# When the taps of the long convolutions enter VectorE's queue: a count of its work in place of a fixed rate

## The chip, the cores and the metric

The kernel runs on one core of a Trainium2 chip. The metric is device time in microseconds (us), the time of one execution; the kernel before was timed three times. A profile of one more execution shows what each engine did.

## What is computed

A decoder trunk of two layers over 1024 positions of 1024 channels, all in float32. Each layer is, cut to what matters here:

```python
h = rmsnorm(x, norm_g)
a_val, a_glu, a_z, qkv, b_z, b_beta, b_alpha, c_u, c_v, c_z, gates = split(h @ w_in)
a   = causal_dwconv(a_val * sigmoid(a_glu), a_dw) + a_dw_b     # 31 taps, 512 channels
y_a = silu(layernorm(a)) * silu(a_z)
q, k, v = split(silu(causal_dwconv(qkv, b_conv)))              # 4 taps, 3072 channels
y_b = rmsnorm(gated_delta_rule(l2norm(q), l2norm(k), v, b_beta, b_alpha)) * silu(b_z)
y_c = gelu(c_u) * spatial_mix(layernorm(gelu(c_v))) * silu(c_z)
merged = sum(sigmoid(gate_i) * (y_i @ proj_i) for i in (a, b, c))
x = x + merged @ w_out
```

## The kernel before

Channels lie on the 128 partitions, positions along the free dimension. A layer has two large parts. The first, which the change touches, makes most of the projection h @ w_in and, beside it, the convolutions and norms. The second runs the delta rule, the remaining gate tiles and the output projections; its code is not touched.

**Pairs, groups, steps.** The first part is the generator `pairs` (L326). A pair is two tiles of 128 projected columns by all 1024 positions, made with Winograd's form of Strassen's method: seven products of half size instead of eight. There are 31 pairs a layer, counted from 0 here. One product is a group: twelve matmuls of 128x512 (four slices of the inner dimension, each in three passes of high and low parts), written to one PSUM tile `ps` of a pool of four (`pg`). Three matmuls with one slice are a step, so a pair has 28 steps; the generator yields after each. After a group, VectorE adds `ps` to the pair's output tiles `o1`, `o2` (L364, one or two adds of 128x512), or ScalarE copies it (L360), and so frees the buffer. After the last group of a pair its `use` function works on the outputs: Tanh and a 1024-wide product for the A branch's GLU (`use_glu`, L1322 and L1323), Silu and two 1024-wide products for the `z` gates (`both` L717, `mul_free` L1137), or the start of a convolution.

**Weights.** Each product needs a weight tile in high and low parts: ScalarE copies the high part (L173), GpSimd subtracts to get the low part (L174) and forms the sums of weights (L287, L298). A buffer for them comes free when TensorE has done the group that used it.

**Convolutions.** The class `Convs` (L652 on) keeps a list of convolutions. A job is one half (512 positions) of one tile: ScalarE begins the running sum in PSUM (L1057 or L706), VectorE adds one tap at a time (L686, the operation called a tap here), ScalarE ends it (L1059 or L708). A tile of the A branch has 60 taps, one of q, k or v 6; 384 a layer. The call `todo.tap()` puts one tap into VectorE's queue.

**What sets the order.** In this part VectorE's and TensorE's instructions stand in the order in which the program writes them (L1414). ScalarE, GpSimd and SyncE are ordered by the scheduler, which estimates when an instruction's inputs are ready. The function `interleave` advances `pairs` by a step and, at steps written down by hand, side generators: the C norm (`c_norm`, `to_norm` L1100 on) and C mix, the gate scalars (`gate_scalars`, L590 on), the A norm (`a_norm`, L1078 on). One norm tile is: TensorE transposes (L1106), VectorE takes statistics (L1067 to L1071), GpSimd an inverse root (L1073), VectorE a small product (L1075), ScalarE the normalising itself (L1109); the transposes back (L1088) or the mix (L1124) follow.

**When a tap is written.** After each step `pairs` adds a credit and writes a tap for each whole credit: 0.65 a step, or 0.5 in the four pairs named as slow (pairs 2, 3, 22 and 23, where the norms run). If there is no convolution at hand, the credit is spent for nothing. So with work at hand the rate is 18.2 taps a pair, whatever else VectorE has to do.

Of the kernel before, what the change touches and what calls it, by code (L numbers as in the profile page):

```python
# [45 lines left out]
S_A_NORM = 8, 5  # L46
S_HEAD = -4, 1
S_NEXT = 50, 61, 77, 76, 74
TAPS_FAST, TAPS_SLOW = 0.65, 0.5
EXTRA = 2  # L50
AT_YC = -20
LAG_DMA, LAG_POOL = 4, 5
# [18 lines left out]
def hybrid_trunk_kernel(ctx: ExitStack, tc: tile.TileContext, x, norm_g, w_in, a_dw, a_dw_b,  # L71
                        a_ln_g, a_ln_b, a_proj, b_conv, b_a_log, b_dt_bias, b_onorm_g, b_proj,
                        c_ln_g, c_ln_b, c_ws, c_bs, c_proj, w_out, final_g, out):
    nc = tc.nc
    PSUM = bass.MemoryType.PSUM
    pe, act, dve, pool, sp = nc.tensor, nc.scalar, nc.vector, nc.gpsimd, nc.sync

    const = ctx.enter_context(tc.tile_pool(name="const", bufs=1))
    prm = ctx.enter_context(tc.tile_pool(name="prm", bufs=1))
# [20 lines left out]
    def F(*ts):  # L100
        for t in ts:
            free.append(held.pop(id(t))[0])
# [220 lines left out]
        made("S4", s2)  # L323
        yield

    def pairs(specs, blk, todo, slow):  # L326

        ws = [{} for _ in specs]
        made = chain(*(blocks(srcs, w, w is ws[-1]) for (srcs, _), w in zip(specs, ws)))
# [3 lines left out]
        with tc.issue_after(last_pow[0].ins), tc.issue_after(last_x[0].ins):  # L333
            for _ in range(len(wfree)):
                make()
        step, credit = 0, 0.0
        for (_, use), w in zip(specs, ws):
            o1, o2 = U("o1"), U("o2")
            c11, c12, c21, c22 = (o[:, h * HALF:(h + 1) * HALF] for o in (o1, o2) for h in range(2))
            last = w is ws[-1]  # L340
            for nm, nb in LAST_STEPS if last else STEPS:
                ps = pg.tile([P, HALF], F32, name="ps")
                wt = w.pop(nm)
                for k in range(4):
                    for i, (wi, ri) in enumerate(PASSES):
                        pe.matmul(ps, lhsT=wt[:, wi, k, :], rhs=blk(nb, ri, k),  # L346
                                  start=(k == 0 and i == 0), stop=(k == 3 and i == 2))
                    step += 1
                    credit += TAPS_SLOW if step // 28 in slow else TAPS_FAST
                    while credit >= 1:  # L350
                        todo.tap()
                        credit -= 1
                    yield
                FW(wt)
                if last:
                    drop_sum(nb)
                with tc.high_priority():
                    alone = dict(A11=c11, S2=c21, A22=c22) if last else dict(A11=c11)
                    if nm in alone:
                        act.activation(out=alone[nm], in_=ps, func=AF.Copy)  # L360
                    else:
                        for out, other in SUMS[nm]:
                            out, other = (dict(C11=c11, C12=c12, C21=c21, C22=c22)[c] for c in (out, other))
                            dve.tensor_tensor(out=out, in0=other, in1=ps, op=ALU.add)  # L364
                    early = {"A11": c11, "S1": c22}.get(nm)
                    if last and early is not None:
                        dve.tensor_tensor(out=c21, in0=c21, in1=early, op=ALU.add)
                    if nm == "S4":
                        use(o1, o2)
                make()  # L370
# [764 lines left out]

    def mul_free(y, u):
        dve.tensor_tensor(out=y, in0=y, in1=u, op=ALU.mult)  # L1137
        F(u)

    def y_rhs(ys):  # L1140
# [140 lines left out]
    def layer(l, before, ws=None, parts=1):  # L1281
# [38 lines left out]
        def use_glu(c):  # L1320
            def use(o1, o2):
                act.activation(out=o1, in_=o1, func=AF.Tanh, scale=0.5)  # L1322
                dve.scalar_tensor_tensor(out=o1, in0=o1, scalar=1.0, in1=o2, op0=ALU.add, op1=ALU.mult)  # L1323
                F(o2)
                a_conv(todo, l, c, o1)
            return use
# [35 lines left out]
        at = {}  # L1362
# [49 lines left out]
        def at_step(nm, d, gap):  # L1412
            return at[nm] * 28 + d, gap
        tc_dve = tc.manual_schedule(engines={mybir.EngineType.DVE})  # L1414
        tc_dve.__enter__()
        slow = (at["c_mix"], at["c_mix"] + 1, at["a_norm"], at["a_norm"] + 1)
        interleave(pairs(specs, block_rhs, todo, slow),
                   [(late(lambda: c_norm(gvs)), *at_step("c_norm", *S_C_NORM)),
                    (late(lambda: c_mix(l, gvs, ys, gus)), *at_step("c_mix", *S_C_MIX)),
                    (late(lambda: gate_scalars(l, r)), *at_step("scalars", *S_SCALARS)),  # L1420
# [177 lines left out]
```

## Time and profile before

| what | value |
|---|---|
| time, median of 3 runs | 2700.17 us (2697.55 to 2701.52) |
| the profiled execution, time | 2699.63 us |
| the profiled execution, span of the core | 2697.9 us |
| mean granted TensorE clock | 0.988 of full speed |
| TensorE matmuls busy | 2576.4 us (95%) |
| VectorE busy | 1653.7 us (61%) |
| ScalarE busy | 1256.4 us (47%) |
| GpSimd busy | 1423.2 us (53%) |

The span runs from the first to the last instruction; the execution's own time is 1.7 us longer. Busy shares are means over parts of the program that differ: the first part of the first layer lies at about 64 to 729 us, that of the second layer at about 1402 to 2060 us. Matmuls follow each other before the one ahead has ended, so their busy times overlap, and the ends are modelled. In a row, PE is TensorE, PEld its weight load, DVE VectorE, ACT ScalarE, POOL GpSimd; "[2.74 <-ACT o L717]" means that the engine was idle for 2.74 us before, and what ended that.

### The profile page before, as it was taken

The page shows a single profiled execution, that of the slowest core. Times are in us where ns is not written, and L with a number is a line of the kernel's source. Part 1 is how long each engine was busy: PE and PEld are TensorE (multiplying, and loading weights), DVE is VectorE, ACT ScalarE, POOL GpSimd, SP SyncE. Part 2 cuts the span into 40 slices and gives each one's busy share as a digit, 9 for nine tenths or more (in the row PEclk, how much of TensorE's full clock was granted, in tenths as well). Part 3 has the DMA queues.
Part 4 walks back from the last instruction along what each step waited for, and adds up shares of the span by engine and source line. Part 5 has one row for each costly group of instructions (what it writes and reads, how often), then busy time and mean ns, then how long its engine had stood idle before and what let it go on. Part 6 is the DMA issues. An engine that isn't in the chain of part 4 may idle for free.

```text
span 2697.9 us, 42676 instructions
## 1 busy us (share of the span) xinstructions
PE 2576.4 (95%) x15963; PEld 2120.3 (79%) x15963; DVE 1653.7 (61%) x2934; ACT 1256.4 (47%) x2996; POOL 1423.2 (53%) x1144
## 2 busy tenths in 40 slices
PE   7899999999899999999999989999998999999998
PEld 6687778878778888788867877888786888877887
DVE  6688998666545453445276888986564545444442
ACT  4433435565556666322134333365654666652221
POOL 7767667767533332363167767676674334224520
PEclk9999999999999999999999999999999999999999
DMA  4122233434544535554312223343446344445432
GB/s 156 47 63 86 87 94 119 139 102 121 178 113 116 146 103 157 184 168 134 117 65 55 71 72 93 94 157 102 125 123 178 104 132 122 123 150 183 156 125 78
DMA packets 361635, 319.65 MB, mean 118 GB/s; under 512 B 98930, under 2 KB 313556, under 8 KB 360404
## 3 DMA queue, kind: packets, MB, share of 16 engines
q1 hardware_dynamic: 361428, 316.92, 38.8%
q8 instruction: 126, 2.06, 0.3%
q14 instruction: 81, 0.66, 0.1%
HBM read 221.12 MB, written 95.75 MB: 117 GB/s over the span
## 4 chain that ended last, share of the span: by engine, by line
PE 79%; DVE 9%; ACT 4%; POOL 3%; DMA 3%; issue 2%; SPq 0%; DVEq 0%; POOLq 0%; ACTq 0%
PE ps L346 35%; PE ps L246 24%; PE ps L1261 6%; PE pa L753 1%; DVE pr L686 1%; PE ps L270 1%; DMA wr<-in_w_in_dram 1%; PE pr L986 1%; PE pr L1003 1%; PE pr L995 1%; POOL S L174 1%; PE pr L1012 1%; DVE nm L1075 1%; DMA gam<-gc_d 1%; PE pa L802 1%
## 5 line engine op out<-in xcount | busy, mean ns | idle before, releaser
L174 POOL TENSOR_TENSOR S<-st,S 128x512 fp32r<-128x512 f32 x248 | 330.6, 1333 | 192.7 <-ACT S L173 192.4
L346 PE MATMUL ps<-hT,A 128*128 128x512 f32 x1488 | 366.0, 394 | 0.0
L686 DVE SCALAR_TENSOR_TENSOR pr<-o,dwT,pr 128x512 f32<-128x512 f32 (+7 forms) x480 | 356.9, 745 | 13.6 <-ACT pr L1057 3.4
L364 DVE TENSOR_TENSOR o<-o,ps 128x512 f32<-128x512 f32 x430 | 287.1, 681 | 116.2 <-PE ps L346 105.9
L174 POOL TENSOR_TENSOR wl<-wr,wh 128x512 fp32r<-128x512 f32 (+2 forms) x164 | 198.5, 1224 | 293.6 <-PE ps L246 138.7
L246 PE MATMUL ps<-hT,wh 128*128 128x512 f32 x960 | 334.4, 429 | 0.0
L346 PEld LDWEIGHTS ps<-hT,A 128*128 128x128 f32 x1488 | 280.9, 190 | 59.0 <-issue 0.8
L173 ACT ACTIVATE S<-st 128x512 fp32r<-128x512 f32 x248 | 156.6, 631 | 359.0 <-PE ps L346 205.0
L174 POOL TENSOR_TENSOR A<-wr,A 128x512 fp32r<-128x512 f32 x186 | 248.8, 1338 | 23.6 <-ACT A L173 23.1
L686 DVE SCALAR_TENSOR_TENSOR pr<-o,cvT,pr 128x512 f32<-128x512 f32 (+3 forms) x288 | 211.7, 751 | 43.3 <-ACT pr L706 39.0
L346 PE MATMUL ps<-T,A 128*128 128x512 f32 x744 | 187.6, 400 | 17.3 <-DVE o L364 17.2
L246 PE MATMUL ps<-hT,wl 128*128 128x512 f32 x480 | 189.5, 395 | 0.0
L346 PE MATMUL ps<-hT,S 128*128 128x512 f32 x744 | 183.8, 392 | 0.0
L346 PEld LDWEIGHTS ps<-T,A 128*128 128x128 f32 x744 | 142.0, 193 | 49.7 <-issue 20.3
L173 ACT ACTIVATE A<-wr 128x512 fp32r<-128x512 f32 x186 | 116.9, 629 | 119.9 <-PE ps L346 109.0
L346 PE MATMUL ps<-T2h,S 128*128 128x512 f32 x496 | 168.4, 397 | 3.0 <-ACT T2h L173 3.0
L346 PE MATMUL ps<-T3h,S 128*128 128x512 f32 x496 | 166.3, 393 | 4.2 <-ACT o L360 4.2
L346 PE MATMUL ps<-T1h,S 128*128 128x512 f32 x496 | 165.2, 392 | 0.0
L173 ACT ACTIVATE wh<-wr 128x512 fp32r<-128x512 f32 (+2 forms) x164 | 85.6, 549 | 165.3 <-issue 123.4
L246 PEld LDWEIGHTS ps<-hT,wh 128*128 128x128 f32 x960 | 151.1, 190 | 11.6
L346 PEld LDWEIGHTS ps<-hT,S 128*128 128x128 f32 x744 | 137.8, 188 | 28.5 <-issue 0.8
L1261 PE MATMUL ps<-woh,mg 128*128 128x512 f32 x512 | 140.7, 391 | 0.0
(298 smaller groups left out, 5732.4 us busy)
## 6 DMA issues: line engine op xcount, KB each, us to landing
wr<-in_w_in_dram SPq DMA_DIRECT2D x160, 512.0 KB
g_d<-gth SPq DMA_DIRECT2D x32, 512.0 KB
g_d<-o SPq DMA_DIRECT2D x16, 512.0 KB
z_d<-o SPq DMA_DIRECT2D x16, 512.0 KB
v_d<-o SPq DMA_DIRECT2D x16, 512.0 KB
k_d<-o SPq DMA_DIRECT2D x16, 512.0 KB
q_d<-o SPq DMA_DIRECT2D x16, 512.0 KB
gam<-gc_d SPq DMA_DIRECT2D x16, 512.0 KB
```

The lines of the kernel that those rows point to most:

```text
L173: act.activation(out=hi, in_=src, func=AF.Copy)
L174: lo_eng.tensor_tensor(out=lo, in0=src, in1=hi.bitcast(F32), op=ALU.subtract)
L246: pe.matmul(ps[h], lhsT=w[wi][:, k, :], rhs=rhs(h, ri, k), start=(k == 0 and i == 0), stop=(k == kt - 1 and i == 2))
L270: pe.matmul(ps[h][:, sl], lhsT=w[wi][:, k, :], rhs=rhs(h, ri, k)[:, sl], start=(k == 0 and i == 0), stop=(k == kt - 1 and i == 2))
L346: pe.matmul(ps, lhsT=wt[:, wi, k, :], rhs=blk(nb, ri, k), start=(k == 0 and i == 0), stop=(k == 3 and i == 2))
L364: dve.tensor_tensor(out=out, in0=other, in1=ps, op=ALU.add)
L686: dve.scalar_tensor_tensor(out=acc[:, lo:], in0=x[:, h * HALF + lo - s:(h + 1) * HALF - s], scalar=taps[s - 1], in1=acc[:, lo:], op0=ALU.m ...
L753: pe.transpose(tp[:, j * P:(j + 1) * P], src[:, half * 4 + j, :], ident)
L802: pe.matmul(tp[:, j], lhsT=kT[:, n], rhs=qT[:, n], start=True, stop=True)
L986: pe.matmul(ks, lhsT=kT[:, n], rhs=st, start=True, stop=True)
L995: pe.matmul(pz, lhsT=zt[:, n, :], rhs=rt, start=True, stop=True)
L1261: pe.matmul(ps[h], lhsT=mg[hh, ri, k // 4][:, k % 4, off:off + P], rhs=wo[k][wi][:, h * HALF:(h + 1) * HALF], start=(k == 0 and i == 0), s ...
```

## The change

The credit goes. In its place the program keeps a count, `queued`, of how much work in us stands in VectorE's queue, by its own reckoning. Every VectorE instruction that is written adds a cost by its kind: 0.68 for a tensor_tensor, 0.75 for a scalar_tensor_tensor (a tap is one), 0.7 for statistics, 0.3 for a reduction, 0.2 for others. The two kinds of 1024-wide products add 1.4 more. Each step of TensorE takes 0.7 off, down to no less than -1.5. Taps are written as long as the count is at or below zero, so at most three at once, and none while other work is counted. The distinction of slow pairs goes too. The count works while the program is built; no instruction is added or removed.

```diff
--- before.py
+++ after.py
@@ -46,7 +46,7 @@
 S_A_NORM = 8, 5
 S_HEAD = -4, 1
 S_NEXT = 50, 61, 77, 76, 74
-TAPS_FAST, TAPS_SLOW = 0.65, 0.5
+STEP_US, IDLE_US, WIDE_US = 0.7, 1.5, 1.4
 EXTRA = 2
 AT_YC = -20
 LAG_DMA, LAG_POOL = 4, 5
@@ -73,7 +73,18 @@
                         c_ln_g, c_ln_b, c_ws, c_bs, c_proj, w_out, final_g, out):
     nc = tc.nc
     PSUM = bass.MemoryType.PSUM
-    pe, act, dve, pool, sp = nc.tensor, nc.scalar, nc.vector, nc.gpsimd, nc.sync
+    pe, act, pool, sp = nc.tensor, nc.scalar, nc.gpsimd, nc.sync
+
+
+    queued = [0.0]
+    COST = dict(tensor_tensor=0.68, scalar_tensor_tensor=0.75, tensor_reduce=0.3, bn_stats=0.7)
+
+    class Counted:
+        def __getattr__(self, name):
+            queued[0] += COST.get(name, 0.2)
+            return getattr(nc.vector, name)
+
+    dve = Counted()
 
     const = ctx.enter_context(tc.tile_pool(name="const", bufs=1))
     prm = ctx.enter_context(tc.tile_pool(name="prm", bufs=1))
@@ -323,7 +334,7 @@
         made("S4", s2)
         yield
 
-    def pairs(specs, blk, todo, slow):
+    def pairs(specs, blk, todo):
 
         ws = [{} for _ in specs]
         made = chain(*(blocks(srcs, w, w is ws[-1]) for (srcs, _), w in zip(specs, ws)))
@@ -333,7 +344,7 @@
         with tc.issue_after(last_pow[0].ins), tc.issue_after(last_x[0].ins):
             for _ in range(len(wfree)):
                 make()
-        step, credit = 0, 0.0
+        queued[0] = 0.0
         for (_, use), w in zip(specs, ws):
             o1, o2 = U("o1"), U("o2")
             c11, c12, c21, c22 = (o[:, h * HALF:(h + 1) * HALF] for o in (o1, o2) for h in range(2))
@@ -345,11 +356,9 @@
                     for i, (wi, ri) in enumerate(PASSES):
                         pe.matmul(ps, lhsT=wt[:, wi, k, :], rhs=blk(nb, ri, k),
                                   start=(k == 0 and i == 0), stop=(k == 3 and i == 2))
-                    step += 1
-                    credit += TAPS_SLOW if step // 28 in slow else TAPS_FAST
-                    while credit >= 1:
-                        todo.tap()
-                        credit -= 1
+                    queued[0] = max(queued[0] - STEP_US, -IDLE_US)
+                    while queued[0] <= 0 and todo.tap():
+                        pass
                     yield
                 FW(wt)
                 if last:
@@ -1135,6 +1144,7 @@
 
     def mul_free(y, u):
         dve.tensor_tensor(out=y, in0=y, in1=u, op=ALU.mult)
+        queued[0] += WIDE_US
         F(u)
 
     def y_rhs(ys):
@@ -1321,6 +1331,7 @@
             def use(o1, o2):
                 act.activation(out=o1, in_=o1, func=AF.Tanh, scale=0.5)
                 dve.scalar_tensor_tensor(out=o1, in0=o1, scalar=1.0, in1=o2, op0=ALU.add, op1=ALU.mult)
+                queued[0] += WIDE_US
                 F(o2)
                 a_conv(todo, l, c, o1)
             return use
@@ -1413,8 +1424,7 @@
             return at[nm] * 28 + d, gap
         tc_dve = tc.manual_schedule(engines={mybir.EngineType.DVE})
         tc_dve.__enter__()
-        slow = (at["c_mix"], at["c_mix"] + 1, at["a_norm"], at["a_norm"] + 1)
-        interleave(pairs(specs, block_rhs, todo, slow),
+        interleave(pairs(specs, block_rhs, todo),
                    [(late(lambda: c_norm(gvs)), *at_step("c_norm", *S_C_NORM)),
                     (late(lambda: c_mix(l, gvs, ys, gus)), *at_step("c_mix", *S_C_MIX)),
                     (late(lambda: gate_scalars(l, r)), *at_step("scalars", *S_SCALARS)),
```

TensorE's instructions stand in the same order as before. On VectorE the taps stand elsewhere; on ScalarE and GpSimd the scheduler places some instructions differently. Line numbers of the changed kernel are higher by 9 to 11 (L364 is L373, L686 is L695, L1137 is L1146, L1322 is L1332). The number in a name like `o_1869` counts buffers and has no meaning across the two.

VectorE at the end of pair 6, in the first layer, before. The two rows with `yc` are the products of `mul_free`, the rows with `pr` taps, those with `ps` adds that free a PSUM buffer:

```order
L686 SCALAR_TENSOR_TENSOR pr<-o_1719,dwT,pr 128x512 x3
L364 TENSOR_TENSOR o_1869<-o_1869,ps 128x512
L1137 TENSOR_TENSOR yc<-yc,o_1869 128x1024
L1137 TENSOR_TENSOR yc<-yc,o_1870 128x1024
L686 SCALAR_TENSOR_TENSOR pr<-o_1719,dwT,pr 128x512 x5
L364 TENSOR_TENSOR o_2029<-o_2028,ps 128x512
```

The same place now:

```order
L695 SCALAR_TENSOR_TENSOR pr<-o_1713,dwT,pr 128x512 x3
L373 TENSOR_TENSOR o_1861<-o_1861,ps 128x512
L1146 TENSOR_TENSOR yc<-yc,o_1861 128x1024
L1146 TENSOR_TENSOR yc<-yc,o_1862 128x1024
L695 SCALAR_TENSOR_TENSOR pr<-o_1713,dwT,pr 128x512
L373 TENSOR_TENSOR o_2021<-o_2020,ps 128x512
```

Between the second product and the next add one tap stands where five stood.

ScalarE from the end of pair 11 on, before. `S_...` and `A_...` are copies of weights for coming groups, the row L1322 is the Tanh of `use_glu`, after which VectorE's 1024-wide product comes:

```order
L173 ACTIVATE S_2823<-st 128x512
L173 ACTIVATE S_2846<-st 128x512
L360 ACTIVATE o_2849<-ps 128x512
L173 ACTIVATE A_2867<-wr 128x512
L173 ACTIVATE S_2887<-st 128x512
L173 ACTIVATE A_2912<-wr 128x512
L1322 ACTIVATE o_2696<-o_2696 128x1024
```

Now:

```order
L184 ACTIVATE S_2823<-st 128x512
L369 ACTIVATE o_2826<-ps 128x512
L184 ACTIVATE A_2842<-wr 128x512
L1332 ACTIVATE o_2670<-o_2670 128x1024
L184 ACTIVATE S_2864<-st 128x512
L184 ACTIVATE A_2889<-wr 128x512
```

The Tanh stands directly behind the first weight copy after L360, ahead of two others that it stood behind. In the C norm GpSimd's root (L1073) of tile 6 stands ahead of the subtraction for an `S` tile that it stood behind, and that of tile 7 ahead of one for an `A` tile; in the A norm the roots of tiles 0 and 1 stand further back by two such instructions, and those of tiles 3 and 4 ahead of a sum (L287, L298) that they stood behind.

VectorE at the first tile of the A norm (pair 22), before; BN_STATS begins the tile's statistics:

```order
L686 SCALAR_TENSOR_TENSOR pr<-o_4280,cvT,pr 128x512 x3
L686 SCALAR_TENSOR_TENSOR pr<-o_4280,cvT,pr 128x511
L364 TENSOR_TENSOR o_4439<-o_4438,ps 128x512
L686 SCALAR_TENSOR_TENSOR pr<-o_4280,cvT,pr 128x510
L1067 BN_STATS bs<-pa 128x6
L1069 BN_AGGR mv<-bs 128x2
L1071 TENSOR_SCALAR ve<-mv 128x1
L1075 SCALAR_TENSOR_TENSOR nm<-mv,lrs 128x1
```

Now:

```order
L695 SCALAR_TENSOR_TENSOR pr<-o_4280,cvT,pr 128x512 x3
L695 SCALAR_TENSOR_TENSOR pr<-o_4280,cvT,pr 128x511
L695 SCALAR_TENSOR_TENSOR pr<-o_4280,cvT,pr 128x510
L695 SCALAR_TENSOR_TENSOR pr<-o_4280,cvT,pr 128x509
L695 SCALAR_TENSOR_TENSOR pr<-o_4281,cvT,pr 128x512 x3
L373 TENSOR_TENSOR o_4439<-o_4438,ps 128x512
L1076 BN_STATS bs<-pa 128x6
L1078 BN_AGGR mv<-bs 128x2
L1080 TENSOR_SCALAR ve<-mv 128x1
L1084 SCALAR_TENSOR_TENSOR nm<-mv,lrs 128x1
```

Nine taps stand between the last add of pair 21 and the statistics, where five stood.

## Rows read from the trace of the kernel before

**Rows 1.** Waits of TensorE, 120:740 us: total us, times, longest us
```profile
PE ps L346 <- DVE o L364: 9.1, 4, 5.4
PE pa L1088 <- ACT acc L1109: 6.3, 4, 2.3
PE pa L635 <- DVE gs L630: 3.2, 1, 3.2
PE pa L1124 <- ACT o L1109: 2.4, 1, 2.4
```

**Rows 2.** The same view, second layer, 1450:2062 us
```profile
PE ps L346 <- DVE o L364: 8.1, 2, 5.3
PE pa L1088 <- ACT acc L1109: 6.0, 4, 2.3
...
PE pa L1124 <- ACT o L1109: 3.0, 1, 3.0
```

**Rows 3.** Timeline, TensorE and VectorE: start us, us, engine, line, operation
```profile
232.58 2.88 PE L346 MATMUL ps<-hT,A 128*128 128x512 f32 x12
...
237.35 4.34 DVE L1137 TENSOR_TENSOR yc<-yc,o 128x1024 f32<-128x1024 f32 x2 [2.74 <-ACT o L717]
...
241.62 3.91 DVE L686 SCALAR_TENSOR_TENSOR pr<-o,dwT,pr 128x512 f32<-128x512 f32 x5
...
245.43 0.68 DVE L364 TENSOR_TENSOR o<-o,ps 128x512 f32<-128x512 f32 x1
```

**Rows 4.** Stretches: busy us (instructions) of PE, PEld, DVE, ACT, POOL; PEclk; DMA
```profile
132.57:137.57 5.00, 5.00 (x19) 4.30 (x20) 4.23 (x10) 2.02 (x5) 1.66 (x2) 0.66 0.00 0
246.26:250.26 4.00, 4.00 (x12) 3.21 (x13) 3.89 (x6) 0.00 (x0) 0.00 (x0) 0.65 0.00 0
279.81:287.81 8.00, 8.00 (x25) 6.70 (x26) 7.08 (x11) 1.85 (x5) 2.55 (x2) 0.57 0.02 5
300.00:340.00 40.00, 40.00 (x178) 33.11 (x178) 39.08 (x59) 15.27 (x22) 29.98 (x24) 1.00 0.34 105
549.00:554.00 5.00, 3.51 (x18) 2.96 (x19) 4.27 (x10) 4.58 (x12) 2.33 (x3) 1.00 0.00 2
1577.33:1581.33 4.00, 4.00 (x12) 3.21 (x13) 3.89 (x6) 0.00 (x0) 0.00 (x0) 0.63 0.00 0
1610.33:1615.33 5.00, 5.00 (x19) 4.25 (x20) 4.93 (x8) 1.72 (x5) 1.04 (x1) 0.66 0.00 0
1685.39:1690.39 5.00, 5.00 (x15) 3.95 (x16) 4.89 (x8) 0.93 (x2) 0.00 (x0) 0.66 0.00 0
1880.51:1885.51 5.00, 5.00 (x17) 4.17 (x18) 4.23 (x10) 4.01 (x10) 1.84 (x2) 0.66 0.00 0
```

**Rows 5.** Groups of VectorE instructions, 64.5:728.7 us: busy, mean ns | idle before
```profile
L686 DVE SCALAR_TENSOR_TENSOR pr<-o,dwT,pr 128x512 f32<-128x512 f32 (+7 forms) x240 | 178.5, 745 | 6.8 <-ACT pr L1057 1.7
```

**Rows 6.** Timeline, ScalarE and VectorE around the end of pair 11
```profile
348.89 1.05 ACT L1322 ACTIVATE o<-o 128x1024 f32<-128x1024 f32 x1
...
349.97 2.30 DVE L1323 SCALAR_TENSOR_TENSOR o<-o,o 128x1024 f32<-128x1024 f32 x1 [5.33 <-ACT o L1322]
```

**Rows 7.** Timeline, VectorE, first and last instruction of the gate scalars' chain
```profile
274.73 1.20 DVE L607 TENSOR_SCALAR beta<-beta 128x64 f32<-128x64 f32 x1
...
279.43 0.23 DVE L630 TENSOR_TENSOR gs<-gs,an 128x64 f32<-128x64 f32 x1
```

**Rows 8.** Timeline, VectorE and GpSimd, C norm, tile 6
```profile
125.35 1.55 POOL L174 TENSOR_TENSOR A<-wr,A 128x512 fp32r<-128x512 f32 x1 [0.68 <-ACT A L173]
...
126.61 0.76 DVE L686 SCALAR_TENSOR_TENSOR pr<-o,dwT,pr 128x512 f32<-128x512 f32 x1 [0.85 <-ACT pr L1057]
...
127.92 1.30 POOL L174 TENSOR_TENSOR S<-st,S 128x512 fp32r<-128x512 f32 x1 [1.01 <-ACT S L173]
...
129.17 0.55 POOL L1073 TENSOR_TENSOR lrs<-ve,mhalf 128x1 f32<-128x1 f32 x1
```

**Rows 9.** Timeline, VectorE, statistics of the A norm's tile 0
```profile
540.60 0.69 DVE L1067 BATCH_NORM_STATS2 bs<-pa 128x6 f32<-128x512 f32 x1
```

## The prediction

> **What bounds the kernel now.** I read first the waits of TensorE, in the stretch of each layer's projections, because TensorE runs nearly without a break there and only what makes it wait can be won. In the first layer it waits 9.1 us in four places for the VectorE adds of L364, 3.2 us once for the last step of the gate scalars, 2.4 us once for the normalised C tiles, and 6.3 us in four places for the normalised A tiles [rows 1]. The second layer shows the same places: 8.1 us in two, 3.0 us, 6.0 us, and 3.2 us for the gate scalars, in a row that reads as in the first [rows 2]. The adds of L364 empty a PSUM buffer; there are four, so a group of twelve matmuls cannot start until the add of the fourth group back is done. All four kinds of wait end in VectorE's queue, or pass through it, and taps stand in that queue between the steps waited for.
>
> Second, the timeline at the longest wait, pair 7 of the first layer. A new group begins at 232.58, so the product of the group before (S2) was complete then; its add starts at 245.43 and takes 0.68 [rows 3]. It is 12.9 us late. In the undisturbed stretch 178 matmuls take 40.00 us [rows 4], so twelve take 2.70 us. Three groups can run meanwhile, 8.1 us; 12.9 + 0.68 - 8.1 = 5.4 us, which is the longest wait of rows 1. An add may thus be some 7.4 us late for nothing. Ahead of it stood the wait for ScalarE's Silu, 2.74 us, two 1024-wide multiplications, 4.34 us, and five taps, 3.91 us [rows 3].
>
> Third, the granted clock behind each wait [rows 4]. [...] A stretch of length L at share c loses L x (1 - c): 1.70, 1.40 and 3.44 us in the first layer, 1.48, 1.70 and 1.70 in the second, together 11.4 us. So a wait is paid once idle and, most times, again slowly.
>
> **The change part by part.** No instruction is added or removed; the 384 taps of a layer stay, the 240 of the long convolution at 0.745 us each [rows 5]. Only their places in VectorE's queue move, and, since ScalarE and GpSimd are ordered by the scheduler, a few instructions there. The counting runs when the program is built and costs nothing on the chip. TensorE's order is the same.
>
> *The adds, 17.2 us (9.1 + 8.1).* After the two multiplications of pair 6 one tap now stands before the next add, where five stood. What is left ahead of that add, counted from the end of pair 6: its last add 0.68, the Silu wait 2.74, the multiplications 4.34 and one tap 0.745, 8.5 us [rows 3, 5]; its own product comes two groups, 5.4 us, after that end, so it is 3.1 us late, under 7.4. That needs the older backlog gone too; it is, because the count lets a tap in only when it stands at zero or less. Does the count drain too fast? A pair of the new order has at most 20 taps and 7 adds. By the busy means that is 20 x 0.745 + 7 x 0.68 = 19.7 us against 28 steps of 0.675, 18.9 us, from the row of 178 matmuls [rows 4, 5]; taken so, the queue grows 0.8 us a pair, 8 us over the ten pairs that are full, of which 7.4 - 3.1 = 4.3 cost nothing. The bounds are 0 and 3.7 us lost a layer. I take 0, since the rows' busy times overlap (the five taps end at 245.53, after the next add's start) and small steps of the norms are over-counted (0.75 for one that works on 128x1). At pair 12 VectorE idles 5.33 us for a Tanh that ScalarE runs at 348.89 [rows 6]; two weight copies stood ahead of it and they wait for TensorE's progress. In the new order it stands ahead of both, so this wait shrinks as well. I take all 17.2 us; the lower bound is the taps alone, 4 x 0.745 = 3.0 us at each of the two longest places, 6.0 us.
>
> *The gate scalars, 6.4 us.* The chain runs from 274.73 to 279.66, 4.9 us [rows 7], and TensorE waited 3.2 us for its end. Three of the eleven taps between the multiplications of pair 7 and the chain leave, 2.2 us, and the older backlog, 12.9 us late at pair 7, goes from 12.9 towards 3.1. With more than 3.2 us gone the wait is over; the next that can be late is ScalarE's Exp and Ln inside the chain, whose length I keep. I take 6.4; bounds 4.4 and 6.4.
>
> *The C norm, 4.4 us of 5.4.* Ahead of tile 6's statistics a tap stood that itself waited 0.85 us for ScalarE and took 0.76 [rows 8]. It is gone. On GpSimd the root of tile 6 now stands ahead of the sum splitting of 1.30 us: it can run when the split that starts at 125.35 ends, 126.90, in place of 129.17, 2.3 us sooner [rows 8]. So of 2.4 and 3.0 us some 0.1 and 0.8 stay; with rounding I take 4.4, bounds 0 and 5.4.
>
> *The A norm, about 2.8 us of 12.3.* Here the change cuts both ways. Before the statistics of tile 0, at 540.60 [rows 9], five taps stood; now nine do, because after an empty stretch the count admits three at once and then one a step. That is 4 x 0.745 = 3.0 us later, and GpSimd's root for it falls behind another split. The first wait of each layer grows, by 2 us as I take it. From tile 3 on, zero to one tap stands between tiles in place of two, and the roots of tiles 3 and 4 pass a sum that they stood behind; I take 3.4 us off the other three waits of a layer. Net 1.4 us a layer. Bounds: 6.0 us lost (two first waits grow by 3.0, nothing else moves) and 12.3 us won.
>
> *The clock.* If the six waits go, so do the six slow stretches: 11.4 us; bounds 0 and, with the one behind the A norm of the second layer, 13.1.
>
> Sum: 17.2 + 6.4 + 4.4 + 2.8 + 11.4 = 42.2 us. The profiled execution took 2699.63 us, 0.5 us under the median of 2700.17, so 2657.4, and against the median 2658.0 us.
>
> [...] The first A-norm wait of either layer is nearly the same (2.3 us is the longest of four in both, rows 1 and 2), yet the clock behind it stays 1.00 in the first layer and falls to 0.66 in the second [rows 4]. So whether a wait is paid twice is partly chance. [...]
>
> **The rivals.** (1) The clock is not given back: the waits that stay (A norm, the last pair, the start) catch the slow stretches. Idle falls 30.8 us, the clock nothing: 2669.4 us. For it speak the two rows above; against it that no low clock appears in a stretch without a wait. (2) The wide operations still come late, because ScalarE and not the taps sets them. Then only 3.0 us go at each of the two longest places and 4.4 at the C norm with its 1.70 of clock: 12.1 us, 2688.1 us. Against it speaks the Tanh's new place. (3) All A-norm waits go with the rest: 9.5 us and 1.70 us more, 2646.8 us. For it speaks that taps thin out from tile 3 on. (4) Slower. The bunching before tile 0 is the rule for all sixteen A-norm tiles: 3.0 us of taps and a split of 1.30 us ahead of each root, 4.3 x 16 = 69 us, against 39.4 won elsewhere: 2730 us. It decides from 39.4 / 16 = 2.5 us a tile. Against it: in the new order only tile 0 has nine taps ahead. (5) The change doesn't do what it says: the count begins at zero and knows nothing of waits, so the backlog builds up all the same, and the time stays 2700 us. Against it stands the order itself.
>
> **How the numbers follow.** The forecast has 0.60, rival 1 0.10, rival 2 0.08, rival 3 0.12, rival 4 0.05, rival 5 0.05. A measurement can tell about 0.2% from no change, 5.4 us. Faster by more are the forecast and rivals 1 to 3, 0.90; within it rival 5, 0.05; slower rival 4, 0.05. The range runs from rival 3, 2647, past rival 1 to 2681, where the bounds of the forecast's own terms meet: the count drains too fast (3.7 us a layer, 7.4), the A norm loses 6.0 in place of winning 2.8 (8.8), and each of these four waits is paid again at the lower clock (4 x 1.70 = 6.8), 23.0 us over 2658. Left out are rivals 2, 4 and 5, 0.18.
>
> **What would show it.** In the waits of TensorE, the rows for L364 (now L373) and for the gate scalars should be gone, or under 1 us together; the row for the C tiles about 1 us; the A norm in one wait of 4 us a layer in place of four. The granted clock should be below 1 only at the start of each layer and perhaps behind the A norm. VectorE's busy time should stay. If the rows for the adds remain and VectorE idles before the wide operations, rival 2 is right; if an L364 wait shows in pairs 13 to 18, the count drains too fast; if the A-norm row grows to 12 us a layer, the bunching outweighs my estimate.

## The result and the profile after

The changed kernel takes 2664.15 us, the median of four runs (2663.13 to 2668.48), against 2700.85 us for the kernel before on the same chip: a ratio of 0.9858, 95% interval 0.9844 to 0.9871, or 36.7 us less. The prediction was 2658, with a range of 2647 to 2681. The profiled execution took 2663.31 us with a span of 2661.5, which is 36.4 us less than the span before.

What TensorE waits for in the stretch of each layer's projections, first layer and then second (engine, line, releaser: total us, times, longest us). The first layer:

```profile
PE pa L1097 <- ACT acc L1118: 5.7, 4, 2.9
PE ps L357 <- ACT o L369: 3.1, 3, 1.7
PE pa L1115 <- ACT o L1118: 0.7, 1, 0.7
PE ps L357 <- ACT o L717: 0.2, 1, 0.2
```

The second layer:

```profile
PE pa L1097 <- ACT acc L1118: 5.6, 4, 2.9
PE ps L357 <- ACT o L369: 3.3, 3, 1.9
...
PE ps L357 <- POOL S L185: 0.5, 1, 0.5
PE ps L357 <- POOL A L185: 0.5, 1, 0.5
```

There is no row any more for the adds (L373 now), the gate scalars or the C mix; before they stood at 17.2, 6.4 and 5.4 us over both layers [rows 1, 2]. The A norm kept its four waits a layer and nearly all of its time: 11.3 us, where it had 12.3. New are two of the three waits for ScalarE's copy L369 in each layer, and small ones near the end.

The place of the longest wait before, pair 7 of the first layer, on the timeline (start us, us, engine, line, operation, in brackets the idle time before and what ended it):

```profile
227.46 4.32 DVE L1146 TENSOR_TENSOR yc<-yc,o 128x1024 f32<-128x1024 f32 x2 [3.35 <-ACT o L726]
...
227.88 2.88 PE L357 MATMUL ps<-hT,A 128*128 128x512 f32 x12
...
231.70 0.74 DVE L695 SCALAR_TENSOR_TENSOR pr<-o,dwT,pr 128x512 f32<-128x512 f32 x1
...
232.35 0.68 DVE L373 TENSOR_TENSOR o<-o,ps 128x512 f32<-128x512 f32 x1
```

The same group of hT and A begins at 227.88, and the add of the product before it starts at 232.35: 4.5 us late, where it was 12.9 [rows 3]. One tap stands behind the two products, not five, and the products begin before the group does, not 4.8 us after it, because the older backlog is gone.

Stretches (us, busy us and instructions of PE, PEld, DVE, ACT, POOL, granted clock, DMA share, GB/s):

```profile
120.00:523.00 403.00, 401.50 (x1816) 332.72 (x1817) 358.26 (x518) 181.82 (x291) 295.36 (x228) 1.00 0.34 101
1432.00:1843.50 411.50, 406.60 (x1842) 336.62 (x1843) 363.82 (x532) 185.90 (x302) 301.00 (x234) 1.00 0.34 102
1843.50:1851.50 8.00, 8.00 (x35) 6.69 (x34) 3.65 (x10) 6.06 (x15) 3.62 (x5) 0.79 0.17 68
2017.60:2025.30 7.70, 7.70 (x36) 6.43 (x35) 4.95 (x7) 4.25 (x10) 4.46 (x5) 0.78 1.06 386
```

The first two rows reach over all the places of the six slow stretches of [rows 4], and the clock is 1.00 throughout. What is left in the pairs, besides the start of each layer (0.54 from 72 to 83 us, 0.50 from 1390 to 1392), lies behind the first wait for the A norm of the second layer, and at the end of that layer's pairs.

The ledger in the profiled executions. In the two stretches of pairs TensorE's idle time falls from 59.5 to 33.6 us, 25.9 less: 30.0 from the four kinds of wait (17.2 + 6.4 + 5.4 + 1.0), less 4.1 of new waits. Both stretches together are 34.5 us shorter, so some 8.6 us, by that difference, come from matmuls that no longer run at a granted clock of 0.50. The kernel before shows 0.50 inside each of the six stretches, from 281 to 286 us for one: there the matmuls of 128x512 begin 0.43 us apart (284.20, 284.63, 285.06); at 1.00 it is 0.23 (320.00, 320.23, 320.45). The rest of the program gives 1.9.

### The profile page after: what moved, and what is told of

Its sections match the earlier page's. It is cut to its first block, busy times and chain, and to the rows that moved or that the text cites. A ratio compares the mean times of both kernels' runs of the same rounds, so it can differ in the third digit from the quotient of the medians.

```text
span 2661.5 us, 42685 instructions
## 1 busy us (share of the span) xinstructions
PE 2568.4 (97%) x15963; PEld 2113.4 (79%) x15963; DVE 1656.7 (62%) x2934; ACT 1256.4 (47%) x2996; POOL 1423.5 (53%) x1144
## 4 chain that ended last, share of the span: by engine, by line
PE 80%; DVE 6%; POOL 4%; ACT 4%; DMA 3%; issue 2%; SPq 0%; DVEq 0%; POOLq 0%; ACTq 0%
PE ps L357 36%; PE ps L257 24%; PE ps L1271 7%; DMA gam<-gc_d 2%; PE pa L762 1%; PE ps L281 1%; POOL S L185 1%; PE pr L1012 1%; PE pr L1004 1%; PE pr L995 1%; POOL st L298 1%; PE pr L1021 1%; DMA wr<-in_w_in_dram 1%; PE pa L811 1%; DVE nm L1084 1%
## 5 line engine op out<-in xcount | busy, mean ns | idle before, releaser
L185 POOL TENSOR_TENSOR S<-st,S 128x512 fp32r<-128x512 f32 x248 | 332.5, 1341 | 166.1 <-ACT S L184 165.7
L695 DVE SCALAR_TENSOR_TENSOR pr<-o,dwT,pr 128x512 f32<-128x512 f32 (+7 forms) x480 | 357.0, 745 | 10.6
L185 POOL TENSOR_TENSOR wl<-wr,wh 128x512 fp32r<-128x512 f32 (+2 forms) x164 | 198.6, 1225 | 293.1 <-PE ps L257 138.7
L373 DVE TENSOR_TENSOR o<-o,ps 128x512 f32<-128x512 f32 x430 | 286.2, 681 | 77.4 <-PE ps L357 66.2
L185 POOL TENSOR_TENSOR A<-wr,A 128x512 fp32r<-128x512 f32 x186 | 253.0, 1361 | 22.3 <-ACT A L184 22.0
L695 DVE SCALAR_TENSOR_TENSOR pr<-o,cvT,pr 128x512 f32<-128x512 f32 (+3 forms) x288 | 213.1, 752 | 48.9 <-ACT pr L715 43.3
```

Source lines behind the costliest of these rows:

```text
L185: lo_eng.tensor_tensor(out=lo, in0=src, in1=hi.bitcast(F32), op=ALU.subtract)
L695: dve.scalar_tensor_tensor(out=acc[:, lo:], in0=x[:, h * HALF + lo - s:(h + 1) * HALF - s], scalar=taps[s - 1], in1=acc[:, lo:], op0=ALU.m ...
```

## The experiments

The ratio of each is to the kernel before, run on the same chip; the changed kernel stands at 0.9858. The first theory, T, is the one of the prediction: the gain comes from taps that no longer stand in VectorE's queue behind long work, and the clock follows the waits.

**The wide products not counted for their width.**

```diff
-STEP_US, IDLE_US, WIDE_US = 0.7, 1.5, 1.4
+STEP_US, IDLE_US, WIDE_US = 0.7, 1.5, 0.0
```

> The changed kernel with the extra 1.4 for each 1024-wide product set to 0: the products still count 0.68 and 0.75, as half as wide work does, and everything else is counted as in the changed kernel. The first theory (T): the time came from keeping taps out behind the wide products, so that the adds behind them stay under 7.4 us late. Then each pair that holds one or two wide products puts 1.4 to 2.8 us more on the queue than is counted; the adds of pairs 6 to 8 come to over 7.4 us late again, rows of TensorE waiting for the L373 adds come back with 3 to 8 us a layer, with 1 to 2 us of half clock behind each, and the time is 2674 to 2690 us. The rival (counting at all, the wide width is beside the point): no such row, 2664 us within 4.

Measured: 2711.36 us, ratio 1.0021 (1.0011 to 1.0032). That is slower than the kernel before, and past T's own range. Waits of the first layer:

```profile
PE pa L644 <- DVE gs L639: 5.1, 1, 5.1
PE pa L1097 <- ACT acc L1118: 5.0, 4, 2.9
PE pa L1133 <- ACT o L1118: 3.6, 1, 3.6
PE ps L357 <- ACT o L369: 3.2, 4, 1.2
PE ps L357 <- DVE o L373: 2.8, 4, 1.8
```

All three kinds that the change had removed are back, gate scalars and C mix larger than in [rows 1]. At this drain the whole of the 36.7 us hangs on counting these products at their width.

**That part alone.** The kernel before, with its fixed rates; only the wide products take credit away (the same line in the Tanh product's code):

```diff
     def mul_free(y, u):
         dve.tensor_tensor(out=y, in0=y, in1=u, op=ALU.mult)
+        credit[0] -= 2.8
```

> The kernel before with its fixed rates of 0.65 and 0.5 kept, and one part of the change alone: each 1024-wide product takes 2.8 taps off the credit (2.08 us at 0.745 us a tap). Norms, gate scalars and adds are not counted. T: the waits for the adds of L364 (17.2 us) go and the half clock behind them with them; the gate scalars and the C norm lie in pairs 2 to 11, whose wide products now hold back some taps there too, so that these two waits (6.2 and 4.8 us) at least halve: 2664 to 2674 us. Rival (all work has to be counted): the waits for gate scalars and C norm stay whole, with the clock behind them: 2677 to 2685 us.

Measured: 2660.66 us, ratio 0.9843 (0.9825 to 0.9860), not to be told from the changed kernel, and 3.3 us below T's range. In both layers the rows for adds, gate scalars and C mix are gone, where T had the last two at least halved. So T's main point holds and its rival falls: norms and gate scalars need not be counted. It is the hold behind the wide products that matters. The chain of the gate scalars starts behind two of them, and a Tanh product stands in the middle of the C norm, at 125.17. Two things changed together there, and no run takes them apart: the kernels without the wait for the C mix have no tap ahead of tile 6's statistics, and its root stands 0.1 us behind them; those with the wait have one or two taps there and the root at 0.8 us or more. The A norm, on the other hand, loses 6.3 us a layer here.

**Only a lower rate.**

```diff
-TAPS_FAST, TAPS_SLOW = 0.65, 0.5
+TAPS_FAST, TAPS_SLOW = 0.55, 0.5
```

> The kernel before with the fixed rate 0.55 in place of 0.65: 15 or 16 taps in a full pair where 18 stood, nothing held back behind wide products. T: behind the two wide products of pair 6 still stand four taps for five, and the older backlog of 1 to 2 us goes, so that the add is some 10 to 11 us late for 12.9 and still waits 2.5 to 4 us for 5.4; the gate scalars wait 2.5 to 3 us for 3.2; the waits of pair 12 and the C norm mostly go: 2678 to 2690 us. Rival (the fixed rate was simply too high, the count does no more than lower it): no row for L364, 2664 us within 5. Below 2660 would mean that a steady rate beats the count.

Measured: 2697.20 us, ratio 0.9984 (0.9975 to 0.9994). Both sides missed. Waits of the second layer:

```profile
PE ps L346 <- ACT o L360: 7.0, 2, 5.7
PE pa L1088 <- ACT acc L1109: 7.0, 4, 3.6
PE pa L635 <- DVE gs L630: 3.5, 1, 3.5
PE pa L1124 <- ACT o L1109: 2.3, 1, 2.3
```

The waits for the adds are gone here too: at pair 7 they are 6.7 us late at most, where T had 10 to 11, because two or three taps fewer a pair also drain the backlog of pairs 5 and 6. But gate scalars and C mix wait as before. The taps that the low rate leaves over, 14 a layer, stand in pair 24, where there were none, and a new wait of 5.7 us for ScalarE's copy L360 appears in pair 25 (3.8 in the first layer). In ScalarE's queue that copy stands behind exponentials of the first head (L785), which wait 5.4 us for GpSimd (4.6). That the taps left over brought ScalarE's order about is not shown: the fastest kernel below has 16 taps in pairs 24 and 25 and no wait there. So a steady rate that is low enough for the adds still leaves the gate scalars and the C mix waiting.

**PSUM buffers in turn.** The four buffers of `pg` become four pools of one, used in turn; every instruction keeps its place on every engine.

> The changed kernel with every instruction in the same place on every engine, only the four PSUM buffers of the projections handed out strictly in turn; in the changed kernel the groups of pairs 15 and 19 take the buffer of the group just before them. T: the two waits of 0.85 us a layer there for the copy of L369 go, and no add is late enough to make a new one (the latest is 7.0 us against 7.4): 3.4 us less, 2661 us, 2659 to 2663. Rival (the reuse is harmless or other groups pay for it, as an add that is 7 us late may now be waited for): 2664 us within 1.5, with a row of waiting for L373.

Measured: 2661.83 us, ratio 0.9850 (0.9833 to 0.9867), too close to call by time. In the trace of the changed kernel the wait looks like this, at pair 19:

```profile
455.19 2.88 PE L357 MATMUL ps<-hT,A 128*128 128x512 f32 x12
458.75 0.50 PE L357 MATMUL ps<-T2h,S 128*128 128x512 f32 x1 [0.69 <-ACT o L369]
```

The group at 458.75 waits for ScalarE to copy out the group that has only just ended, so it reuses that group's buffer. In turn, these four waits are gone, as T had it; but a new one of 1.0 us comes in each layer at pair 20, where an add is now 8.4 us late. The rival was half right: most of it is paid elsewhere.

**Not counted for width, and a slower drain.** As the first experiment, with `STEP_US` 0.66.

> The changed kernel with the extra 1.4 of the wide products at 0, as in the earlier run without it, and the count drained by 0.66 a step in place of 0.7: 18 or 19 taps in the full pairs where that run had 20 or 21. It splits that run's slowness (2711 us) in two. T (the wide products, undercounted, put a queue ahead of gate scalars, C norm and adds in pairs 2 to 9, whatever the drain): these waits stay at two thirds or more of what that run shows (gate scalars 5.1, C norm 3.6 and adds 2.8 to 4.7 us a layer) and the time is 2695 to 2710 us. Rival (the drain of 0.7, faster than VectorE works, built that queue): under a third of them stays, 2664 to 2675 us.

Measured: 2686.99 us, ratio 0.9945 (0.9930 to 0.9960), between the two. First layer:

```profile
PE pa L644 <- DVE gs L639: 3.2, 1, 3.2
PE ps L357 <- DVE o L373: 2.8, 2, 1.8
PE pa L1133 <- ACT o L1118: 2.5, 1, 2.5
```

Of the first experiment's waits for gate scalars, C mix and adds about two thirds stay (17.2 of 25.1 us over both layers), which is T's mark, yet 24 us of time go. Both parts are real: the missing width (30 us against the next run, which drains at 0.67), and a drain of 0.7 that is faster than TensorE's own 0.675 us a step (178 matmuls in 40.00 us [rows 4], three to a step).

**Counted for width, drained by 0.67.**

```diff
-STEP_US, IDLE_US, WIDE_US = 0.7, 1.5, 1.4
+STEP_US, IDLE_US, WIDE_US = 0.67, 1.5, 1.4
```

> The changed kernel with the count drained by 0.67 a step in place of 0.7, which is less than the 0.675 us that a step takes in the row of 178 matmuls. T: the adds of pairs 12 to 19, up to 6.8 us late in the changed kernel, come within 3 us; no group takes the buffer of the group before it, so the four waits of 0.85 us in pairs 15 and 19 go; 10 to 20 taps a layer move behind pair 20, towards the norm of A, whose first wait grows by 0 to 2 us. 2660 to 2664 us. Rival (a queue short of 7.4 us costs nothing, and later taps only collide with the norm of A and with the heads): 2664 to 2670 us.

Measured: 2657.35 us, ratio 0.9830 (0.9816 to 0.9845): about 7 us under the changed kernel, with intervals that just touch. From pair 13 to pair 19 the adds are at most 2 us late (6.8 in the changed kernel), and the first layer has two rows left over 0.5 us:

```profile
PE pa L1097 <- ACT acc L1118: 5.5, 4, 2.8
PE ps L357 <- ACT o L369: 1.8, 1, 1.8
```

The time is 2.7 us below T's range: the A norm lost nothing by the taps that moved towards it. TensorE idles 6.4 us less over both layers' pairs than in the changed kernel. The four waits at pairs 15 and 19 are 2.8 us of that; the rest is spread over small waits and was not followed.

**A hold ahead of the A norm.**

```diff
+        def hold():
+            queued[0] += 4.5
+            yield
...
+                    (late(hold), *at_step("a_norm", S_A_NORM[0] - 6, 1)),
                     (late(lambda: a_norm(l, accs)), *at_step("a_norm", *S_A_NORM)),
```

> The changed kernel with one more hold: 4.5 us are added to the count six steps ahead of the norm of A, so that the five taps that stand in the changed kernel just ahead of its first statistics (3.78 us) go behind the norm. T, as in the prediction (taps in the queue ahead of the statistics make the first wait): the first wait of each layer, 2.9 us, falls to under 1 us, with the half clock behind it in the second layer: 2656 to 2660 us. Rival: the chain goes through GpSimd, whose power of 0.55 us stands behind a weight sum of 1.3 us in its queue, and through ScalarE; VectorE's part is not what ends it: the first wait changes by under 1 us, 2662 to 2667 us.

Measured: 2658.24 us, ratio 0.9838 (0.9823 to 0.9853). First and second layer:

```profile
PE pa L1097 <- ACT acc L1118: 1.7, 3, 0.7
```

```profile
PE pa L1097 <- ACT acc L1118: 2.7, 3, 1.7
```

The first wait, 2.9 us, is gone in both, and the granted clock stays at 1.00 behind it in the second layer. New waits of 0.8 us in the first layer and 2.5 us in the second stand in pair 25. T's numbers hold; that its reason holds does not follow, as the last two experiments show.

**One place alone.** The kernel before, with `credit[0] -= 2.8 * (pair[0] == 6)` behind the wide products.

> The kernel before with taps held back by 2.8 behind each wide product of pair 6 alone, all else at the fixed rates: some five taps of one pair in each layer move. T: the waits for the adds in pair 7 (5.5 and 5.4 us lost) go, with the half clock behind them (1.4 and 1.5 us), and the queue of 4 to 5 us that this takes away is missing in pairs 8 and 9 too, so that the gate scalars' wait of 3.3 us shrinks; the waits of pairs 2 and 12 stay. 12 to 20 us less than before: 2682 to 2690 us. Rival (the backlog only moves on, and the next thing in the queue waits in its place; the clock is not given back): the waits for the adds of pair 7 go, others grow, 2693 to 2703 us.

Measured: 2691.20 us, ratio 0.9956 (0.9939 to 0.9972), 1.2 us over T's range. First layer:

```profile
PE pa L1090 <- ACT acc L1111: 6.1, 3, 4.4
PE pa L637 <- DVE gs L632: 5.1, 1, 5.1
PE ps L348 <- DVE o L366: 2.6, 4, 1.7
```

The wait of pair 7 falls from 5.4 to 1.7 us, but the gate scalars' grows from 3.2 to 5.1 and the first of the A norm from 2.3 to 4.4. So T's second half was wrong: the queue did not get shorter for pairs 8 and 9. Adds in pair 8 are up to 13.6 us late here, 12.6 before. The likely reason is that TensorE's own wait in pair 7 had been the pause in which VectorE caught up. The clock is not given back either, as the rival had it (the mean granted clock is 0.985 to 0.988 in four executions, 0.984 to 0.986 before): the slow stretches behind pair 7 are gone, but behind the first wait for the A norm the granted clock is 0.57 over 8 us in both layers (544 and 1872 us), where before it stayed at 1.00 in the first layer.

**Two edits together: 0.67 and the hold of 4.5.**

> The changed kernel with two of the earlier edits together: the count drained by 0.67 a step, and 4.5 us added to it six steps ahead of the norm of A. T (the two act in different places, pairs 12 to 20 and pair 22, and their gains add): against the run with 0.67 alone (2657 us) the first wait for the norm of A goes, 2.85 and 2.46 us, and with it one stretch of half clock of 3.4 us or more at 1843 or 528 us: 2649 to 2653 us. Rival (the 384 taps have to be done by pair 25 in any case; what is held back here ends in pairs 24 and 25, in front of the adds and heads there): waits for L373 or L369 of 2 to 6 us in pair 25, as in the run with the rate 0.55, and 2655 to 2662 us.

Measured: 2649.75 us (2648.64 to 2650.79), ratio 0.9806 (0.9792 to 0.9821): the fastest, 51.5 us under the kernel before, with an interval clear of the changed kernel's. The gains add, and no wait comes in pair 25. The one in pair 26, 0.2 us in the changed kernel, grows to 1.1 and 1.8.

**The same with 0.68.**

> The same with 0.68 in place of 0.67, which is more than the 0.675 us of a step, so that more taps are done before the norm of A and fewer are left behind it. T: the queue of the full pairs grows by at most 0.14 us a pair and costs nothing; the first wait for the norm of A is gone; 2649 to 2655 us. Rival of the run before (taps left for pair 25): smaller waits there than with 0.67, so that this kernel is the faster of the two by 2 us or more.

Measured: 2664.15 us, ratio 0.9862 (0.9845 to 0.9880). Both sides missed: 14.4 us slower than 0.67, and the first wait for the A norm is back. VectorE's statistics are done at 520.66, GpSimd's root L1082 comes at 522.72:

```profile
520.51 0.15 DVE L1080 TENSOR_SCALAR ve<-mv 128x1 f32<-128x1 f32 x1
```

```profile
520.23 1.30 POOL L298 TENSOR_TENSOR st<-st,wr 128x512 f32<-128x512 f32 x1
521.48 1.29 POOL L185 TENSOR_TENSOR A<-wr,A 128x512 fp32r<-128x512 f32 x1
522.72 0.55 POOL L1082 TENSOR_TENSOR lrs<-ve,mhalf 128x1 f32<-128x1 f32 x1
```

With 0.67 the root stands ahead of both weight instructions:

```profile
519.79 0.56 POOL L1082 TENSOR_TENSOR lrs<-ve,mhalf 128x1 f32<-128x1 f32 x1
520.31 1.31 POOL L298 TENSOR_TENSOR st<-st,wr 128x512 f32<-128x512 f32 x1
521.57 1.31 POOL L185 TENSOR_TENSOR A<-wr,A 128x512 fp32r<-128x512 f32 x1
```

Here GpSimd took its instructions in the order of its queue: the split L185 of 521.48 begins ahead of the root, whose input was there at 520.66. The scheduler sets that order by its estimate of when VectorE will be ready, and a few taps more or less ahead go with another order.

The first wait is only 4.6 of the 14.4 us. TensorE idles 10.7 us more over both layers' pairs than with 0.67, and waits for ScalarE's copy L369 in pair 25, 2.1 and 2.7 us, which are not there with 0.67, count as much. As with the rate 0.55, that copy stands in ScalarE's queue behind exponentials of the first head (L794) that wait for GpSimd, 5.3 us in the first layer. With the hold of 4.5, then, a drain of 0.67, 0.68 and 0.7 gives 2650, 2664 and 2658 us: the orders on the other engines count for more here than the drain.

The new theory for the first wait: GpSimd's order, not VectorE's queue, decides it. The last two kernels were to part this theory from the first.

**Taps away, one weight sum still ahead of the root** (0.7 a step, a hold of 6.0, nine steps ahead).

> The run with 0.68 and the hold kept its first wait for the norm of A (2.4 us a layer), and two things stood ahead of the first tile there: four taps on VectorE, and two weight sums of 1.3 us on GpSimd ahead of the first power. This kernel and the next take them apart. Here: the changed kernel (0.7 a step) with 6.0 us added to the count nine steps ahead of the norm, so that one tap stands ahead of the first statistics, where the changed kernel has nine in a row, while on GpSimd one weight sum (L298) that the run with the hold at 0.7 has behind the first power still stands ahead of it. Taps theory: the first wait is under 0.5 us. GpSimd theory: 1.2 to 2.4 us of it stay. In time: 2656 to 2660 us against 2659 to 2664 us.

Measured: 2660.85 us, ratio 0.9846 (0.9832 to 0.9861); the first wait stays whole at 2.9 us in both layers, more than the GpSimd theory had; the time is within its range. VectorE begins the statistics at 520.13, 0.04 us after the transposes end, so the taps have no part in the first tile's delay. GpSimd:

```profile
520.54 1.30 POOL L185 TENSOR_TENSOR S<-st,S 128x512 fp32r<-128x512 f32 x1
521.92 1.30 POOL L298 TENSOR_TENSOR st<-st,wr 128x512 f32<-128x512 f32 x1
523.16 0.56 POOL L1082 TENSOR_TENSOR lrs<-ve,mhalf 128x1 f32<-128x1 f32 x1
```

The statistics were ready at 521.23; the root waited 1.9 us. One tap still stands between the first two tiles.

**Taps there, the root early** (0.67 a step, a hold of 3.0, ten steps ahead).

> The other half: 0.67 a step, and 3.0 us added to the count ten steps ahead of the norm of A. Three taps stand ahead of the first statistics and one more ahead of the second, against two and none in the run with 0.67 and 4.5, while on GpSimd both weight sums stand behind the first power, as in that run. Taps theory: 1.0 to 2.5 us of the first wait stay, 2652 to 2658 us. GpSimd theory: it is under 0.5 us, 2648 to 2652 us.

Measured: 2653.09 us, ratio 0.9809 (0.9796 to 0.9823), in the range of the taps theory and 1.1 us above the other's. The first wait is gone in the second layer and about 1.2 us in the first, so neither theory holds whole. Nor are the taps tested as was meant: VectorE is done with the three and idles 2.7 us before the last add ahead of the statistics, which begin directly behind the transposes. In both layers one tap stands between the first two tiles. What differs is the length of tile 1's small product L1084, in the first layer and in the second:

```profile
524.36 1.24 DVE L1084 SCALAR_TENSOR_TENSOR nm<-mv,lrs 128x1 f32<-128x1 f32 x1 [0.66 <-POOL lrs L1082]
```

```profile
1833.93 0.16 DVE L1084 SCALAR_TENSOR_TENSOR nm<-mv,lrs 128x1 f32<-128x1 f32 x1 [0.66 <-POOL lrs L1082]
```

That is 1.1 of the 1.2 us; the last section shows when the product is long.

**What ends the first wait.** In every run that has it, TensorE goes on 0.05 to 0.06 us after ScalarE has normalised tile 1, not tile 0. In the changed kernel, ScalarE and then TensorE:

```profile
529.47 1.51 ACT L1118 ACTIVATE acc<-pa,nm,lrs 128x128 f32<-128x128 f32 x4 [2.05 <-DVE nm L1084]
```

```profile
531.03 0.66 PE L1097 MATMUL pa<-ident,acc 128*128 128x128 f32 x4 [2.90 <-ACT acc L1118]
```

The program has two PSUM buffers `pa`; tile 2's transposes take the one that tile 0 held, and the transposes back need the one that tile 1 held. So the delays along the chain of both tiles add up: taps ahead of tile 0's statistics, its root and its product, taps and adds ahead of tile 1's statistics, its root and its product. The root of tile 0 alone does not decide. In the kernel before with only the hold behind the wide products (**That part alone**), the statistics of tile 0 begin directly behind the transposes, and the root stands 0.1 us behind them; still the first wait is 3.3 us in both layers. Three taps stand between the two tiles:

```profile
521.58 1.40 DVE L688 SCALAR_TENSOR_TENSOR pr<-o,cvT,pr 128x512 f32<-128x512 f32 x2
...
523.50 0.74 DVE L688 SCALAR_TENSOR_TENSOR pr<-o,cvT,pr 128x510 f32<-128x510 f32 x1
524.15 0.69 DVE L1069 BATCH_NORM_STATS2 bs<-pa 128x6 f32<-128x512 f32 x1
```

Tile 1's root stands another 1.0 us behind a weight instruction there, and its product takes 1.21 us. In the two kernels with the hold of 4.5 that lose the wait (0.7 and 0.67), no tap stands between the tiles, tile 0's root is at most 0.6 us behind its statistics, and tile 1's product takes 0.16 us. What each term alone is worth was not measured.

## Why the prediction was right, and where its steps were off

- **The adds** (17.2 expected, 17.2 found). The queue in pair 7 came out nearly as worked: 4.5 us late for 3.1, 0.6 of it because VectorE idled 3.35 us for the Silu rather than 2.74, and most of the rest because the last add of pair 6 began 1.0 us behind its product. Rival 2, that ScalarE sets the time of the wide products, is out. The experiments without the width and with the width alone show the cause.
- **Does the count drain too fast?** It does. Between pairs 13 and 19 the adds' delay rises from 3.6 to 6.1 us, 0.4 a pair; I had a bound of 0.8 and took 0. It stays under the 7.4 us that are free, so the step stood. But the 7.4 rested on "there are four, so a group of twelve matmuls cannot start until the add of the fourth group back is done". That is not so: at pairs 15 and 19 a group took the buffer of the group just before it. Four waits of 0.7 us were not in the sum.
- **Gate scalars** (6.4 expected, 6.4 found) and **C norm** (4.4 of 5.4 expected, 5.4 found): right.
- **The A norm** (2.8 expected, 1.0 found). The first waits grew by 0.6 and 0.8 us, not 2, and the other three of a layer lost 1.1, not 3.4. The failed step is to price the first wait by tile 0 alone, by the taps ahead of its statistics ("4 x 0.745 = 3.0 us later") and its root. The statistics did come 2.5 us later. But the wait ends with tile 1. On the way there, in the first layer, the two products L1084 took 0.16 us each for 1.24 and 1.21, and one tap fewer stood between the tiles, 2.8 us less in all; tile 1's root stood 1.2 us behind a weight sum. That the wait grew so little is a balance of terms that the prediction did not have.
- **The clock** (11.4 expected). All six named stretches are at 1.00 now, and the one behind the A norm stayed. Why the clock falls behind one wait and not behind another is not shown: the first wait for the A norm is 2.9 us in both layers of the changed kernel, and the clock behind it is 1.00 in the first and 0.79 over 8.00 us in the second. In the ledger it is 8.6 us in the pairs, partly because a slow stretch now lies inside the second layer's pairs, at 2017.60 (0.78 over 7.7 us, 1.7 us). Rival 1 is out. Two readings were off: the rows show seven slow stretches, of which the sum takes six, and in the second layer the wait of 2.3 us is the third for the A norm; its first is 2.1.
- **The sum**: 42.2 expected, 36.4 found in the profiled executions. The difference is 1.8 at the A norm, 4.1 in waits that are new, and 2.8 at the clock, less 1.0 more at the C norm and 1.9 in the rest of the program, for which there was no term.

What stays open: what the tap and the root are each worth in the C norm; what orders ScalarE's queue in pair 25; and the remaining three waits of the A norm, 2.7 and 2.8 us in the fastest kernel. Moving the root off GpSimd was not tried.

## What to carry to other kernels

Background work that shares an in-order queue should be let in by what already stands there, with the long instructions at their true length, and drained by about the measured time of the pacing engine's step. Here that is 0.675 us (178 matmuls in 40.00 us, three to a step); 0.67 was about 7 us faster than 0.7, but with the hold 0.68 was 14 us slower than 0.67, so the value is to be tried out. A wait in one place can also be the pause in which a queue drains, so that its removal alone gives back less than its length. And after the queue of one engine has been cleared, read the in-order queues of the others on the same chain: a small urgent instruction may stand behind bulk work there only because a scheduler's estimate moved.

## What the hardware showed that was not expected

The small VectorE product L1084 (128x1, both inputs in SBUF) has two durations. In the fastest kernel, at the first two tiles of the A norm:

```profile
520.38 1.25 DVE L1084 SCALAR_TENSOR_TENSOR nm<-mv,lrs 128x1 f32<-128x1 f32 x1 [1.09 <-POOL lrs L1082]
...
523.91 0.16 DVE L1084 SCALAR_TENSOR_TENSOR nm<-mv,lrs 128x1 f32<-128x1 f32 x1 [0.66 <-POOL lrs L1082]
```

The first starts 0.07 us after GpSimd's L298 of 520.31 and ends 0.01 us behind it; the second starts at 523.91, when GpSimd is idle (its root ends at 523.87). In the changed kernel 22 of the 32 such products start while a GpSimd instruction runs, take 1.23 to 1.27 us, and end 0.01 to 0.02 us behind that instruction; the other ten take 0.16. The taps, which read one input from PSUM, do not show it: the 369 with GpSimd busy throughout take 0.748 us in the mean there, the 102 with GpSimd idle 0.749. The wide products do. Two of them took 4.32 us in the changed kernel's pair 7 above, with GpSimd busy for all of it. Two earlier ones, with GpSimd busy for 0.65 us beside them, took 2.61:

```profile
166.97 2.61 DVE L1146 TENSOR_TENSOR yc<-yc,o 128x1024 f32<-128x1024 f32 x2 [1.67 <-ACT o L726]
```

In the kernel before with only the hold behind the wide products, the two of pair 7 took 2.60:

```profile
225.64 2.60 DVE L1139 TENSOR_TENSOR yc<-yc,o 128x1024 f32<-128x1024 f32 x2 [1.51 <-ACT o L719]
```

So the count's 2.08 us for a wide product is near its length beside GpSimd, 4.32 over two. Why these lengths go with GpSimd's work is not shown. That they do means that GpSimd's order can cost the A norm twice: where the root stands, and what runs when the product behind it starts.
